# Expert weights of a two-block transformer kernel in another HBM layout

## The chip, the cores and the metric

The kernel runs on one core of one Trainium2 chip, in float32 throughout; many products are made of two float32r parts. The metric is the device time of one execution in microseconds, the median of several. PE is TensorE, ACT ScalarE, DVE VectorE, POOL GpSimd and SP SyncE. A row names a line of the kernel as L963, and the releaser of a wait stands behind an arrow.

## What is computed

The reference chains two transformer blocks over 256 tokens of width 1024. The first has two kinds of attention heads, a mixture of 32 experts with 4 chosen per token, and an embedding gate; the second has block attention, a linear recurrence and a feed-forward net. The part that the change touches is the mixture of experts:

```
logits = xt @ w_router + b_router;  top_logit, top_e = lax.top_k(logits, 4);  gate = softmax(top_logit)
# per expert e, over the tokens xs that chose it:
hh = jnp.dot(xs, w_gu[e]) + b_gu[e]                    # (1024, 2048) weights
glu, lin = jnp.split(hh, 2, axis=-1)                   # clipped at 7
act = glu * jax.nn.sigmoid(1.702 * glu) * (lin + 1.0)
y = jnp.dot(act, w_dn[e]) + b_dn[e]                    # (1024, 1024) weights, then times gate and summed per token
```

Every expert's weights are 12.6 MB, so all 32 together are 403 MB of the 480 MB that the kernel reads.

## The kernel before

**Stages.** First mixer (to about 150 us), routing (to 165), experts (to about 1118), embedding gate and second mixer (to about 1260), feed-forward net (to the end).

**Weights as a stream.** All large weights come in chunks of up to 2 MB, a tile of 128 partitions with 16 KB each. `plan` (L165 on, filled by `want`) lists them in the order of use: for expert `e` four chunks `("gu", e, c)`, then the two chunks `("dn", e - 1, c)` of the expert before it. `load_next` (L213) takes the next entry and issues its transfer on SP's queue; two chunks of the last experts go over POOL's queue (L228), and the very last as two halves (L231). `done(key)` is called when the last matmul of a chunk stands in the program; it gives the buffer back and calls `load_next` for the same ring. Three rings hold the buffers: `ringa` with three, `ringb` with five until expert 30, `ringc` with one, so nine chunks can be landed or under way. A transfer waits on SP until its buffer is free, and SP handles the plan in order.

The chunks of `w_gu` and `w_dn` are cut out of the weights as the reference has them, by rearranged views:

```
wg = A["w_gu"].rearrange("e (c k p) n -> e c p k n", p=P, k=2)   # L182: partition p gets rows p and 128 + p, 8 KB each
wd = A["w_dn"].rearrange("e (c k p) n -> e c p k n", p=P, k=4)   # L183: four rows, 4 KB each
```

Other weights (`w_in`, `w_in2`, `w_up`) are already permuted on the host, in `host_arrays`, so that a partition's 16 KB are one run.

**An expert on the engines.** `gather` (L939 to L951) picks the expert's up to 64 tokens by a one-hot product; `up` (L963) makes 64 matmuls over the four gu chunks, two column halves of the array at a time; ACT copies the result out, `glu` (L978) transposes it and DVE and ACT apply the gate; `down` (L999) makes 32 matmuls over the two dn chunks; `scatter` (L1027) adds the rows back to the tokens. The loop runs the `up` of expert e + 1 before the `down` of expert e. `past_slots` (L1056) stands between `up` and `down` of the last experts: a branch on the largest count of tokens (L1059, L1060) around a loop that reloads weights in small pieces for tokens past the 64 slots.

The order of instructions on each engine is drawn up when the program is built, by a planner that orders by priority and by estimated durations; `tc.issue_after` pins it in a few places, none in the loop over experts up to expert 29.

Of the kernel before, what the change touches and what calls it, by code (L numbers as in the profile page):

```python
# [36 lines left out]
P = 128  # L37
S = 256
D = 1024
# [9 lines left out]
# ---------------------------------------------------------------- constants of the shapes  # L49
# [3 lines left out]
def _const_pack():  # L53
    cols, parts, at = {}, [], 0

    def put(name, a):
        nonlocal at
        a = np.asarray(a, np.float32)
        cols[name] = (at, a.shape[1])
        parts.append(a)  # L60
        at += a.shape[1]

    i = np.arange(P)
    r, c = i[:, None], i[None, :]
    put("ident", r == c)
    put("flip", r + c == P - 1)
    put("iotad", np.broadcast_to(c % CAP, (P, P)))
    put("iota32", np.broadcast_to(np.arange(E)[None, :], (P, E)))
    put("comb", (r < 64) & (r % 32 == c % 32))
    put("masksb", np.where(c >= r, NEG, 0.0))  # L70
    put("maskml", np.where(c > r, NEG, 0.0))
    put("upper", r < c)
    # distance 255 - m of a row of the relative bias, m = 0 .. 383
    n = np.arange(384)
    dist = 255 - n
    nn = np.maximum(dist, 0)
    nf = np.maximum(nn, 1).astype(np.float32)
    large = 16 + (np.log(nf / np.float32(16)) / np.float32(math.log(8.0)) * np.float32(16)).astype(np.int32)
    bucket = np.where(nn < 16, nn, np.minimum(large, 31))
    oh = np.zeros((P, 384), np.float32)  # L80
    oh[bucket, n] = 1.0
    oh[:, dist < 0] = 0.0
    put("bucket", oh)
    put("maskd", np.broadcast_to(np.where(dist < 0, NEG, 0.0)[None, :], (P, 384)))
    return cols, np.ascontiguousarray(np.concatenate(parts, axis=1))
# [6 lines left out]
# columns of the per-partition vectors  # L92
# [11 lines left out]
def block_kernel(ctx: ExitStack, tc: tile.TileContext, A, out, dbg=None, parts=("t1", "moe", "over", "t3")):  # L104
# [36 lines left out]
    # ------------------------------------------------------------ constants  # L141
# [22 lines left out]
    # ------------------------------------------------------------ weights that stream  # L164
# [17 lines left out]
    wg = A["w_gu"].rearrange("e (c k p) n -> e c p k n", p=P, k=2)  # L182
    wd = A["w_dn"].rearrange("e (c k p) n -> e c p k n", p=P, k=4)  # L183
# [63 lines left out]
    # ------------------------------------------------------------ helpers  # L247
    def split(pool, src, tag="w", eng=V):
        """src in two float32r parts."""
        shape = [P] + list(src.shape[1:])  # L250
        hi = pool.tile(shape, FR, name=tag + "h")
        lo = pool.tile(shape, FR, name=tag + "l")
        act(hi, src)
        eng.tensor_tensor(out=lo, in0=src, in1=hi.bitcast(FT), op=OP.subtract)  # L254
        return hi, lo

    def tiles_T(key):
        """the column tiles of a transposed product: (chunk key, half, tile)."""
        return [(key, hf, m) for hf in range(2) for m in range(2)]
# [25 lines left out]
    def sq_mean(o, src, junk):  # L285
        """the share of 512 columns in the mean of 1024 squares."""
        act(junk, src, AF.Square, scale=1.0 / 32.0, accum_out=o)
# [7 lines left out]
    def rms_halves(o, src, small, junks=None):  # L295
        """1 / rms of the rows of src [128, 1024]."""
        ss = small.tile([P, 2], FT, name="ss2", bufs=4)
        for n in range(2):
            junk = junks(n) if junks else small.tile([P, 512], FT, name="junk", bufs=2)
            sq_mean(ss[:, n:n + 1], src[:, n * 512:(n + 1) * 512], junk)  # L300
        rs_sum(o, ss, small)

    def turn_tile(src, t, gcol, uh, ul, psum):
        """one token tile [128, 1024] transposed, times the gain column of each k tile, in two parts."""
        tl = slice(t * P, (t + 1) * P)
        for g in range(2):
            pt = psum()
            for k in range(4):
                PE.transpose(pt[:, k * P:(k + 1) * P], src[:, (4 * g + k) * P:(4 * g + k + 1) * P], ident)
            for k in range(4):  # L310
                kk = 4 * g + k
                pk = pt[:, k * P:(k + 1) * P]
                if k % 2 == 0:
                    act(uh[:, kk, tl], pk, AF.Copy, scale=gcol(kk))
                else:
                    ts(uh[:, kk, tl], pk, gcol(kk), None, OP.mult)
                stt(ul[:, kk, tl], pk, gcol(kk), uh[:, kk, tl].bitcast(FT), OP.mult, OP.subtract)

    def spread_tile(rB, r, t, small, psum):
        """rB [128, 256]: the column r of one token tile along the free axis, on every partition."""  # L320
        rb = small.tile([P, P], FT, name="rb", bufs=1)
        ts(rb, ones, r[:, t:t + 1], None, OP.mult)
        pb = psum()
        PE.matmul(pb[:, 0:P], rb, ident, start=True, stop=True)
        V.tensor_copy(rB[:, t * P:(t + 1) * P], pb[:, 0:P])
# [9 lines left out]
    # ============================================================ first mixer  # L335
# [31 lines left out]
    # constants that are not needed at once  # L367
# [12 lines left out]
    # ---- projections of the stick-breaking heads  # L380
# [46 lines left out]
    # rotary tables  # L427
# [30 lines left out]
    # ---- stick-breaking heads, and the latent projections between them  # L458
# [6 lines left out]
    def pair_out(o, which, p, gname):  # L465
        """the two parts of a pair of heads times its gain, and their squares."""
        k = 4 * which + p
        sq = t1l.tile([P, S], FT, name="sq", bufs=2)
        act(sq, o, AF.Square)
        act(mxh[:, k], o, AF.Copy, scale=vc(gname, p))  # L470
        stt(mxl[:, k], o, vc(gname, p), mxh[:, k].bitcast(FT), OP.mult, OP.subtract)
        if p == 0:
            sqs[which] = psc.tile([P, 2], FT, name="c")
        for t in range(2):
            PE.matmul(sqs[which][:, t:t + 1], sq[:, t * P:(t + 1) * P], ones[:, 0:1], start=(p == 0 and t == 0),
                      stop=(p == 3), skip_group_check=True)
        if p == 3:
            for t in range(2):
                rsq(hcol[:, 2 * which + t:2 * which + t + 1], sqs[which][:, t:t + 1], 512, t1l)
# [67 lines left out]
    # latent projections  # L547
# [7 lines left out]
    def latent(nk, ncol, gname, dst, wsplit_iter, last_done):  # L555
        """tokens by ncol, normalised, transposed into dst."""
# [49 lines left out]
    def mla_proj():  # L606
# [14 lines left out]
        # queries  # L621
# [48 lines left out]
    # half of -8 softplus(-lam)  # L670
# [10 lines left out]
    # rows of the relative bias by distance; the router's weights times their gain  # L681
# [19 lines left out]
    # ---- latent heads  # L701
# [39 lines left out]
    def half_o(which):  # L741
        """the product of one half of w_o, scaled by its norm."""
# [33 lines left out]
    # ============================================================ routing  # L776
# [30 lines left out]
    # the tokens transposed, for the router  # L807
# [46 lines left out]
    def gate_values():  # L854
# [13 lines left out]
        # what goes past the slots  # L868
# [23 lines left out]
    # three bfloat16 parts that add up to the tokens  # L892
# [30 lines left out]
    # ============================================================ experts  # L923
# [132 lines left out]
    def past_slots():  # L1056
        """pairs past the slots of their expert."""
        pacc = pc_.tile([P, 512], FT, name="sc")
        mv = nc.values_load(maxi[0:1, 0:1], min_val=0, max_val=S)  # L1059
        with tc.If(mv > CAP):  # L1060
            with ExitStack() as c5:
# [12 lines left out]
                with tc.For_i(0, E, 1) as e:  # L1074
                    cv = nc.values_load(cnti[0:1, ds(e, 1)], min_val=0, max_val=S)
                    with tc.If(cv > CAP):
                        with ExitStack() as c4:
# [6 lines left out]
                            for m in range(8):  # L1084
                                w = ov.tile([P, 8, 2, P], FT, name="ovw", bufs=2)
                                for s in range(2):
                                    SY.dma_start(w[:, :, s], A["w_gu"][ds(e, 1), :, s * 1024 + m * P:s * 1024 + (m + 1) * P]
                                                 .rearrange("o (k p) n -> p (o k) n", p=P))
# [13 lines left out]
                            for s in range(4):  # L1102
                                w = ov.tile([P, 8, 256], FT, name="ovw", bufs=2)
                                SY.dma_start(w, A["w_dn"][ds(e, 1), :, s * 256:(s + 1) * 256]
                                             .rearrange("o (k p) n -> p (o k) n", p=P))
# [37 lines left out]
    # the last two experts' rows meet in one accumulation  # L1143
# [20 lines left out]
    def row_split(key, i, gain=None):  # L1164
        """a k tile of weights, times the gain column, in two parts."""
# [19 lines left out]
    # ============================================================ gate of the embeddings, final norm  # L1185
# [8 lines left out]
    def nat2(keys, lhs, epilogue, pre, gain=None):  # L1194
        """[tokens, 1024] = lhs^T w; the last four k tiles go token tile by token tile."""
# [46 lines left out]
    def norm_rows(t, src, gain, o, res, last=None, part=None):  # L1242
        """rows of src normalised, times the gain row, added to res."""
# [61 lines left out]
    # ============================================================ second mixer  # L1305
# [46 lines left out]
    def lru_a(hf):  # L1352
        # r = (1 + tanh) / 2, log a = c8 r; 1 - a^2 = tanh(-log a) (1 + a^2)
# [198 lines left out]
    # ============================================================ feed forward  # L1552
# [68 lines left out]
# ---------------------------------------------------------------- host: layout only  # L1621
def host_arrays(inputs):
# [10 lines left out]
    def colchunks(a, n):  # L1633
        """(1024, m*n) -> [m][128][8*n]"""
# [3 lines left out]
    def pairs(a, n=256):  # L1638
        """chunks of two halves: [m/2][128][2][8*n]"""
# [3 lines left out]
    def rows(a):  # L1643
        """(1024, 512) -> [1][128][2][4*512]"""
# [24 lines left out]
    f["w_gu"] = c(g["w_gu"][0])  # L1669
    f["w_dn"] = c(g["w_dn"][0])  # L1670
# [60 lines left out]
```

## Time and profile before

| | us |
|---|---|
| median of the runs (lowest, highest) | 1460.15 (1459.87, 1460.45) |
| span of the profiled execution | 1458.6 |
| PE busy | 1346.5 (92%) |
| DVE busy | 633.4 (43%) |
| ACT busy | 370.8 (25%) |
| POOL busy | 40.5 (3%) |
| DMA, mean over the span | 330 GB/s |

The page gives no time of the profiled execution beside its span; the span stands 1.55 us under the median of the runs. The busy time of an engine is the union of its instructions. The DMA share is the mean over 16 DMA engines of the time that their packets took; packets can overlap, so it can exceed 1. The granted clock of PE is a share of its full 2.4 GHz; the lower level is 1.2 GHz.

### The profile page before, as it was taken

Reading aid. Unit: us, or ns where it says so; the run is one execution under the profiler, and the core shown is the slowest. Engines: PE = TensorE matmul, PEld = TensorE weight load, DVE = VectorE, ACT = ScalarE, POOL = GpSimd, SP = SyncE. Lnnn points to the kernel's source line nnn. Section 1 sums busy time; section 2 is a strip of 40 time slices with the busy share of each in tenths; the row PEclk is TensorE's granted clock in tenths of the full one; section 3 lists DMA queues with packets and bytes.
Section 4 is the critical chain, followed back from the end, with each engine's and each line's share of the span. In section 5 each row is a group of like instructions: output and inputs, shape, how many; then the busy total and the mean of one; then the engine's idle time right before and its main releaser. Section 6 shows DMA issues by size and latency. Waiting matters only on the chain. (4 is left out here: it accounts for less than half of the span.)

```text
span 1458.6 us, 19750 instructions
## 1 busy us (share of the span) xinstructions
PE 1346.5 (92%) x8361; PEld 747.0 (51%) x8362; DVE 633.4 (43%) x1250; ACT 370.8 (25%) x639; POOL 40.5 (3%) x54
## 2 busy tenths in 40 slices
PE   6999999999999999999899889899897999999997
PEld 6877533433333333333333333333333897799997
DVE  5676422332233223322332223222224878777776
ACT  5545210100100010001000010000113647465554
POOL 1010200000000000000000000000000101000000
PEclk9999999999999999999999999999999999999999
DMA  7238799999999999999999999999997543344540
GB/s 276 109 129 365 280 417 417 415 415 417 417 417 415 416 417 416 418 415 416 417 416 418 415 416 417 416 417 415 405 385 304 196 175 131 118 186 183 201 165 29
DMA packets 82380, 481.91 MB, mean 330 GB/s; under 512 B 4104, under 2 KB 5792, under 8 KB 46448
## 3 DMA queue, kind: packets, MB, share of 16 engines
q1 hardware_dynamic: 79616, 472.93, 80.4%
q0 software_dynamic: 1808, 6.55, 1.2%
q8 instruction: 67, 1.10, 0.3%
q10 hardware_dynamic: 864, 1.13, 0.3%
q14 instruction: 25, 0.20, 0.0%
HBM read 479.53 MB, written 1.06 MB: 329 GB/s over the span
## 5 line engine op out<-in xcount | busy, mean ns | idle before, releaser
L963 PE MATMUL gu<-w,xg 128*64 128x512 f32 x2048 | 476.3, 616 | 16.4 <-DMA w<-w_gu 15.8
L963 PEld LDWEIGHTS gu<-w,xg 128*64 128x64 f32 x2048 | 143.8, 141 | 312.6 <-issue 275.9
L999 PE MATMUL y<-w,gl 128*64 128x512 f32 x1024 | 238.7, 603 | 9.4 <-PEq L1060 6.1
L120 ACT ACTIVATE h<-gu,gs 128x512 f32<-128x512 f32 x64 | 40.5, 683 | 579.6 <-PE gu L963 579.6
L254 DVE TENSOR_TENSOR wl<-w,wh 128x1024 fp32r<-128x1024 f32 (+2 forms) x124 | 148.0, 1205 | 46.8 <-ACT wh L120 46.3
L120 ACT ACTIVATE wh<-w 128x1024 fp32r<-128x1024 f32 (+2 forms) x125 | 128.1, 1038 | 96.5 <-PE acc L272 21.0
L123 DVE TENSOR_TENSOR xg<-xg,vec 128x512 f32<-128x512 f32 x32 | 22.1, 691 | 283.1 <-PE gu L963 279.8
L999 PEld LDWEIGHTS y<-w,gl 128*64 128x64 f32 x1024 | 69.6, 137 | 129.5 <-issue 121.1
L123 DVE TENSOR_TENSOR h<-sc,h 128x512 f32<-128x512 f32 x126 | 81.6, 686 | 117.2 <-PE sc L1027 113.5
L271 PE MATMUL wk<-ul,wh 128*128 128x256 f32 x336 | 94.5, 281 | 0.2 <-DVE ul L123 0.2
L270 PE MATMUL wk<-uh,wh 128*128 128x256 f32 x336 | 94.5, 281 | 0.0
L272 PE MATMUL wk<-uh,wl 128*128 128x256 f32 x336 | 94.3, 281 | 0.0
L126 DVE SCALAR_TENSOR_TENSOR sg<-y,gs,li 128x512 fp32r<-128x512 f32 x31 | 23.3, 751 | 125.2 <-ACT li L120 125.2
L120 ACT ACTIVATE li<-y,gs 128x512 fp32r<-128x512 f32 x31 | 21.3, 687 | 194.1 <-PE y L999 194.1
L939 PEld LDWEIGHTS <-u 128*128 128x128 bf16 x1536 | 54.3, 98 | 28.0 <-issue 27.4
L271 PEld LDWEIGHTS wk<-ul,wh 128*128 128x128 f32 x336 | 63.4, 189 | 1.2 <-DVE ul L123 0.4
L270 PEld LDWEIGHTS wk<-uh,wh 128*128 128x128 f32 x336 | 63.3, 188 | 1.0 <-ACT uh L120 0.2
L272 PEld LDWEIGHTS wk<-uh,wl 128*128 128x128 f32 x336 | 63.4, 189 | 0.0
L978 PE MATMUL tr<-cf,h 128*128 128x128 f32 x256 | 39.3, 286 | 23.6 <-ACT h L120 23.4
L939 PE MATMUL xg<-oh,u 128*128 128x64 bf16 x1536 | 59.6, 193 | 0.7 <-ACT proj L120 0.7
L123 DVE TENSOR_TENSOR gl<-tr,bgu 128x512 f32<-128x512 f32 x32 | 22.1, 691 | 71.3 <-PE tr L978 71.3
L978 PEld LDWEIGHTS tr<-cf,h 128*128 128x128 f32 x256 | 26.8, 140 | 51.3 <-ACT h L120 49.2
(410 smaller groups left out, 1750.8 us busy)
## 6 DMA issues: line engine op xcount, KB each, us to landing
w<-w_gu SPq DMA_DIRECT2D x128, 2048.0 KB, 25.9
w<-w_dn SPq DMA_DIRECT2D x61, 2048.0 KB, 30.7
w<-w_up SPq DMA_DIRECT2D x11, 2048.0 KB, 8.9
w<-w_in SPq DMA_DIRECT2D x7, 2048.0 KB, 10.3
w<-w_down SPq DMA_DIRECT2D x5, 2048.0 KB, 7.4
w<-w_o SPq DMA_DIRECT2D x4, 2048.0 KB, 8.9
w<-w_dn POOLq DMA_DIRECT2D x2, 2048.0 KB, 14.4
w<-w_pg SPq DMA_DIRECT2D x2, 2048.0 KB, 9.3
```

What stands on the lines that cost most here:

```text
L120: return SC.activation(out=o, in_=i, func=f, **kw)
L123: return V.tensor_tensor(out=o, in0=a, in1=b, op=op)
L126: return V.scalar_tensor_tensor(out=o, in0=a, scalar=s, in1=b, op0=op0, op1=op1)
L254: eng.tensor_tensor(out=lo, in0=src, in1=hi.bitcast(FT), op=OP.subtract)
L270: PE.matmul(o, l[0], r[0], start=first, stop=False)
L271: PE.matmul(o, l[0], r[1], start=False, stop=False)
L272: PE.matmul(o, l[1], r[0], start=False, stop=last)
L939: PE.matmul(px[:, kd], u3[i][:, t, kd * P:(kd + 1) * P], oh[:, t], start=(n == 0), stop=(n == 5))
L963: PE.matmul(ps[64 * s:64 * s + 64, n], xg[:, k], w[:, kk, s * 1024 + n * 512:s * 1024 + (n + 1) * 512], start=(k == 0), stop=(k == 7))
L978: PE.transpose(pt[:, m], hf[:, m * P:(m + 1) * P], ident)
L999: i = PE.matmul(ps[64 * s:64 * s + 64], aT[:, k], w[:, kk, s * 512:(s + 1) * 512], start=(k == 0), stop=(k == 7))
```

## The change

The host permutes `w_gu` and `w_dn` into chunks as they lie in SBUF: `w_gu` becomes (32, 4, 128, 2, 2048), `w_dn` (32, 2, 128, 4, 1024). The two rearranged views in the kernel fall away, and each chunk's transfer reads one run of 16 KB per partition. `past_slots` reads small pieces of the same weights by expert and column; each of its transfers is split by chunk (four for `w_gu`, two for `w_dn`). Comments are removed and leave empty lines. Nothing else differs.

```
-    wg = A["w_gu"].rearrange("e (c k p) n -> e c p k n", p=P, k=2)
-    wd = A["w_dn"].rearrange("e (c k p) n -> e c p k n", p=P, k=4)
+    wg, wd = A["w_gu"], A["w_dn"]
...
                                 for s in range(2):
-                                    SY.dma_start(w[:, :, s], A["w_gu"][ds(e, 1), :, s * 1024 + m * P:s * 1024 + (m + 1) * P]
-                                                 .rearrange("o (k p) n -> p (o k) n", p=P))
+                                    for c in range(4):
+                                        SY.dma_start(w[:, 2 * c:2 * c + 2, s],
+                                                     wg[ds(e, 1), c, :, :, s * 1024 + m * P:s * 1024 + (m + 1) * P]
+                                                     .rearrange("o p k n -> p (o k) n"))
...
-                                SY.dma_start(w, A["w_dn"][ds(e, 1), :, s * 256:(s + 1) * 256]
-                                             .rearrange("o (k p) n -> p (o k) n", p=P))
+                                for c in range(2):
+                                    SY.dma_start(w[:, 4 * c:4 * c + 4], wd[ds(e, 1), c, :, :, s * 256:(s + 1) * 256]
+                                                 .rearrange("o p k n -> p (o k) n"))
...
-    f["w_gu"] = c(g["w_gu"][0])
-    f["w_dn"] = c(g["w_dn"][0])
+    f["w_gu"] = c(g["w_gu"][0].reshape(E, 4, 2, P, 2 * D).transpose(0, 1, 3, 2, 4))
+    f["w_dn"] = c(g["w_dn"][0].reshape(E, 2, 4, P, D).transpose(0, 1, 3, 2, 4))
```

## Rows read from the trace of the kernel before

**Rows 1.** The page: span, and GB/s in 40 equal slices.

```profile
span 1458.6 us, 19750 instructions
...
GB/s 276 109 129 365 280 417 417 415 415 417 417 417 415 416 417 416 418 415 416 417 416 418 415 416 417 416 417 415 405 385 304 196 175 131 118 186 183 201 165 29
```

**Rows 2.** Stretches: length, engines' busy us (instructions), PEclk, DMA share, GB/s.

```profile
300.00:700.00 400.00, 374.28 (x2304) 145.61 (x2300) 117.47 (x245) 35.46 (x55) 0.00 (x0) 0.97 1.02 416
700.00:1030.00 330.00, 293.47 (x1792) 111.95 (x1790) 93.62 (x194) 28.40 (x44) 0.00 (x0) 0.98 1.02 416
```

**Rows 3.** The page's DMA issues: count, KB each, us to landing.

```profile
w<-w_gu SPq DMA_DIRECT2D x128, 2048.0 KB, 25.9
```

**Rows 4.** Waits of PE, 200 to 703 us (all), then 703 to 1073 (longest).

```profile
PE sc L1027 <- ACT li L120: 12.6, 16, 0.8
PE tr L978 <- ACT h L120: 12.6, 15, 0.8
PE y L945 <- DVE sg L126: 4.7, 17, 0.3
...
PE gu L963 <- DMA w<-w_gu: 15.8, 18, 2.9
```

**Rows 5.** Timeline of PE: start, us, instructions; first chunk of experts 7, 8, 9.

```profile
355.22 3.65 PE L963 MATMUL gu<-w,xg 128*64 128x512 f32 x16
...
383.37 5.35 PE L963 MATMUL gu<-w,xg 128*64 128x512 f32 x16
...
413.19 3.65 PE L963 MATMUL gu<-w,xg 128*64 128x512 f32 x16
```

**Rows 6.** Stretches around the long chunk of expert 8.

```profile
366.00:383.30 17.30, 15.39 (x118) 6.76 (x114) 5.46 (x11) 2.58 (x4) 0.00 (x0) 1.00 1.01 416
383.40:388.70 5.30, 5.30 (x20) 1.46 (x18) 1.75 (x6) 0.00 (x0) 0.00 (x0) 0.68 1.03 410
```

**Rows 7.** Timeline of PE: chunks of experts 19, 24, 24, 25 and 30.

```profile
703.11 3.65 PE L963 MATMUL gu<-w,xg 128*64 128x512 f32 x16
...
855.25 3.65 PE L963 MATMUL gu<-w,xg 128*64 128x512 f32 x16
...
868.33 3.65 PE L963 MATMUL gu<-w,xg 128*64 128x512 f32 x16 [1.33 <-DMA w<-w_gu]
...
885.36 5.35 PE L963 MATMUL gu<-w,xg 128*64 128x512 f32 x16
...
1037.57 3.65 PE L963 MATMUL gu<-w,xg 128*64 128x512 f32 x16
```

**Rows 8.** Timeline of PE, 1050 to 1103 us: expert 30, then the branch.

```profile
1050.64 3.65 PE L963 MATMUL gu<-w,xg 128*64 128x512 f32 x16 [1.34 <-DMA w<-w_gu]
...
1060.99 3.65 PE L999 MATMUL y<-w,gl 128*64 128x512 f32 x16 [0.93 <-DMA w<-w_dn]
...
1102.78 5.88 PE L999 MATMUL y<-w,gl 128*64 128x512 f32 x14 [6.07 <-PEq L1060]
```

**Rows 9.** Stretches of one run length: w_gu (8 KB), then w_o (4 KB).

```profile
120.00:140.00 20.00, 20.00 (x114) 14.63 (x114) 13.94 (x42) 11.17 (x33) 0.00 (x0) 1.00 1.01 422
...
79.00:83.00 4.00, 4.00 (x31) 3.51 (x30) 2.71 (x7) 1.49 (x4) 0.00 (x0) 0.88 1.00 410
```

**Rows 10.** Stretches of w_in (16 KB), and the packets from 15 to 23 us.

```profile
15.00:23.00 8.00, 7.54 (x38) 7.15 (x39) 4.82 (x13) 7.45 (x16) 1.11 (x2) 1.00 1.01 429
...
16.00:22.00 6.00, 5.97 (x27) 5.89 (x28) 3.18 (x9) 5.45 (x13) 1.11 (x2) 1.00 1.00 426
...
DMA packets 229, 3.43 MB, mean 429 GB/s; under 512 B 19, under 2 KB 19, under 8 KB 19
```

**Rows 11.** Timeline of PE: first chunks of experts 1 and 2.

```profile
185.71 13.95 PE L963 MATMUL gu<-w,xg 128*64 128x512 f32 x64
...
211.86 13.95 PE L963 MATMUL gu<-w,xg 128*64 128x512 f32 x64
```

**Rows 12.** A stretch in which w_in's transfers run beside others.

```profile
1130.00:1135.00 5.00, 5.00 (x23) 4.09 (x23) 4.59 (x4) 3.50 (x4) 0.39 (x1) 1.00 0.98 357
```

## Prediction

> **What bounds the kernel now.** The page comes first. It gives the profiled execution a span of 1458.6 us, 1.55 us under the 1460.15 us median of the runs; I take what lies around the span as constant, so a step that shortens the span by x takes x off the median. The slices of the page show one long middle, 23 of 40, at 415 to 418 GB/s [rows 1]: the expert stage. There the stretches read a DMA share of 1.02 at 416 GB/s, first half and second half alike, with PE busy for 374 of 400 us and then 293 of 330 [rows 2]. So both resources are nearly full, and the question is which of them ends last. A w_gu chunk needs 25.9 us from issue to landing [rows 3] though its 2 MB take 5 us at that rate: some five chunks stand in the queue, and the transfers never pause.
>
> The waits decide it. Between 200 and 703 us PE waits for ACT and DVE alone, never for a weight; between 703 and 1073 us it waits for w_gu 18 times [rows 4]. The stage therefore has two halves with different bounds. In the first, PE paces itself: expert 7 begins at 355.22, expert 8 at 383.37, expert 9 at 413.19 [rows 5], periods of 28.15 and 29.82 us. The two differ by one chunk of 16 matmuls that takes 5.35 us where others take 3.65: over 383.4 to 388.7 the granted clock is 0.68, a piece at 1.2 GHz among 2.4 GHz, after 17.3 us in which PE was busy for 15.4 at a clock of 1.00 [rows 5, 6]. That falls in every second expert from the sixth to the eighteenth, so PE's own pace is a mean of 28.99 us per expert. In the second half DMA sets the pace: expert 24 begins at 855.25, expert 25 at 885.36, 30.11 us, with a wait of 1.33 us for w_gu inside [rows 7].
>
> Why the waits start only at expert 19: nine ring buffers are full when the experts begin, and PE, faster than the stream by 30.25 - 28.99 = 1.26 us per expert, eats that stock. (30.25 us is one expert's 12.583 MB at 416 GB/s.)
>
> **The change, part by part.** *The plan's views* lose their rearrange: the same 192 chunks of 2 MB, same order, same buffers, same 128 partitions; each partition's 16 KB is one run where it was two of 8 KB (w_gu) or four of 4 KB (w_dn). No instruction is added or removed outside the branch of past_slots. *past_slots* gets 52 more DMA instructions in a body that this input doesn't enter: no load of it stands in the trace, and the 6.07 us that PE idles at that branch [rows 8] stay; between nothing and 0.5 us for a longer jump, and I take nothing. *The host* permutes before the launch: outside the time.
>
> What a run's length is worth on the chip has three readings in this trace. A stretch of w_gu chunks alone, 120 to 140 us, moves 422 GB/s; w_o chunks in 4 KB runs move 410 GB/s [rows 9]. The w_in chunks at the start already lie with 16 KB per partition: 15 to 23 us moves 429 GB/s, 16 to 22 us 426. In those 8 us 229 packets carry 3.43 MB, and 19 of them are under 512 B: the other 210 are 16.3 KB each, so a 16 KB run does go as one packet, and under a full queue [rows 10]. I take 429, the longer stretch, with 426 as the lower end; above it the trace shows nothing, and as will be seen a higher rate would not show in the time. At 429 GB/s an expert's 12.583 MB take 29.33 us (29.54 at 426) against 30.25 before: 0.92 us per expert, 0.153 us per chunk.
>
> The Trainium skill's page "DMA: Bandwidth & Descriptors", section "Why small descriptors are slow (HBM only)", speaks against so much: it gives a fixed overhead of about 3 cycles per packet and finds packing worthwhile only at descriptors of 256 B or less. By its figures (32 B per cycle, 850 MHz) an expert's packets would take 0.96% less, an estimate from that page, 0.29 us per expert in place of 0.92, and the kernel would come out near 1451 us, as at the lower rate of the second rival. The trace's steps from 410 to 422 to 429 GB/s are larger than that rule allows.
>
> Now who uses the 0.92 us. A faster stream can't speed PE where PE doesn't wait, so experts 0 to 18 stay as they are and expert 19 still begins at 703.11 [rows 7]. From there PE can run at its own pace: 11 periods to expert 30, six of 28.15 and five of 29.82, 318.0 us, so expert 30 begins at 1021.1 in place of 1037.57 [rows 7]: **16.5 us**. Inside expert 30 the waits of 1.34 us for w_gu and 0.93 us for w_dn [rows 8] go too: **2.3 us**. Together 18.8 us.
>
> Does the stream keep up with that? Its hardest point is expert 30's last w_gu chunk, which PE waited for at 1050.64 [rows 8]. At its own pace PE wants it at 1021.1 + 11.2 = 1032.3 (the three chunks before it and the scatter among them, 3.65 us each and 0.66), 18.3 us sooner. About 168 chunks flow without a pause before it, so each has to gain 0.109 us: a rate of 425 GB/s is enough. At 429 the chunk lands 168 x 0.153 = 25.7 us sooner, 7.4 us ahead of need; at 426 just in time. So of 25.7 us only 18.8 show: DMA stops being what ends last, and PE's pace takes its place. Behind expert 30 I find no wait of the tail for w_gu or w_dn, so it moves forward whole.
>
> Forecast: span 1458.6 - 18.8 = 1439.8, time 1460.15 - 18.8 = **1441.4 us**.
>
> **The rivals.** *One, PE's order changes.* The order of instructions is drawn up when the program is built, by a planner with estimated durations, and another layout may change its estimates. The experts are not all ordered alike: expert 1 to expert 2 took 185.71 to 211.86, 26.15 us [rows 11], with the gather placed where it hides PE's waits for ACT. If that order came to hold throughout, DMA would stay the bound and all 25.7 us and the 0.93 would show: 1433.5 us. Against it: bytes, count and order of the loads stay the same. 8%.
>
> *Two, the run's length is worth less.* If a 16 KB run goes no faster than an 8 KB one, only w_dn gains: 6 chunks at 422 GB/s are 29.82 us per expert, 0.072 us per chunk, 12.0 us by expert 30's last chunk; with the 0.93 that is 1447 us. At 420 GB/s it is 8.1 and 0.93: 1451 us. The same comes out if the change doesn't do what it says and the long run is cut into 8 KB packets; the 16.3 KB per packet speak against it. 12%.
>
> *Three, long packets get in each other's way under load: slower.* In 1130 to 1135 us, where w_in's 16 KB packets run beside other loads, a DMA share of 0.98 moves only 357 GB/s [rows 12]: an expert would take 35.2 us, a chunk 0.83 us more than now, and 168 of them 140 us: some 1600 us. It decides as soon as the rate falls below 416 GB/s. Against it: loads start on idle engines in that stretch, and the stretch at a full queue [rows 10] shows no such thing. 3%.
>
> *Four, PE's pace gets worse* (an order with one more wait for ACT, or the low clock in every expert). The low clock in all 11 would give 328.0 in place of 318.0 us, a gain of 8.8: 1451; an order worse by 1.5 us per expert would eat all of it. 7%, more than half of it within 0.2% of now or slower.
>
> **How the numbers follow.** The forecast has 70%. Its own lower end: without any fall of the clock the 11 periods are 309.7 us, a gain of 27.1 us, of which the stream allows 26.6: 1433.5 us. The range runs from 1433 to 1450: it takes in the forecast, rival one and the better half of rival two, and leaves out the other half, three and four. About 0.2% (3 us) is what a measurement of this kernel can tell from no change. Faster 0.91, same 0.05, slower 0.04.
>
> **What would show it.** Right: about 429 GB/s between 300 and 700 us; some 24,700 packets for w_gu and w_dn where their runs now make 65,500; no wait of PE for either; expert 19 beginning near 703 as before; periods of 28.15 and 29.8 us up to expert 30; and a stock that lasts, so that chunks land before they are wanted. Wrong: waits for w_gu that remain after 900 us (the step of the rate), experts before 19 that begin at other times (the step of the order), a rate at or under 422 (rival two), a period other than 28.15 without a wait or a low clock (rival four).

## The result and the profile after

The changed kernel takes 1438.1 us (median of 4 runs, 1437.8 to 1439.1) where the kernel before takes 1460.3: a ratio of 0.985, 95% interval 0.984 to 0.987. The forecast was 1441.4 us, in a range of 1433 to 1450. Two further measurements of the same two kernels on other chips gave 0.988 (0.985 to 0.990) and 0.986 (0.985 to 0.987). Between the medians the three gains are 22.2, 19.6 and 21.2 us, against the 18.8 forecast. Of the 12 executions of the changed kernel the two fastest (1435.0 and 1435.4 us) show a mean granted clock of 0.981 and the two slowest (1443.5 and 1443.7) one of 0.975, so gains that differ by two or three us may differ by the clock alone. The profiled execution of after took 1437.77 us, 1.77 of them around its span.

From the page of the changed kernel: the span, the engines' busy time, GB/s in 40 slices, all packets, and the packets of SP's queue (count, MB, share of the 16 engines).

```profile
span 1436.0 us, 19750 instructions
PE 1342.9 (94%) x8361; PEld 748.1 (52%) x8362; DVE 633.5 (44%) x1250; ACT 371.0 (26%) x639; POOL 40.1 (3%) x54
...
GB/s 281 111 126 375 275 428 426 428 427 426 427 426 427 427 427 427 426 427 428 426 427 426 427 428 426 426 429 426 395 382 306 176 150 132 132 181 199 200 154 30
DMA packets 41549, 481.92 MB, mean 336 GB/s; under 512 B 4104, under 2 KB 5792, under 8 KB 13680
...
q1 hardware_dynamic: 39552, 472.93, 79.5%
```

The same queue's row on the page of before:

```profile
q1 hardware_dynamic: 79616, 472.93, 80.4%
```

The same bytes, and 40,064 packets fewer; with the 768 that POOL's queue saved (1808 before, 1040 after) it is 40,832. That is 32 experts x 16 DMA engines x 80 (128 packets per engine and expert before, 48 after) less 128, which are the pieces of 8 KB in which the very last chunk, issued as two halves, still goes. So the long runs did go as one packet each. The long middle of the slices stands at 426 to 428 GB/s where it stood at 415 to 418 [rows 1].

Two stretches of the middle (length, busy us of PE, PEld, DVE, ACT and POOL, PEclk, DMA share, GB/s), to be laid beside [rows 2]:

```profile
300.00:700.00 400.00, 373.25 (x2296) 145.35 (x2292) 117.96 (x246) 36.14 (x56) 0.00 (x0) 0.97 1.01 427
700.00:1000.00 300.00, 280.81 (x1710) 109.45 (x1712) 88.95 (x187) 25.81 (x40) 0.00 (x0) 0.97 1.01 427
```

In the first, PE is as busy as before (373 of 400 us, 374 before): there it gained nothing from the faster stream. The second is the one that changed: 94% busy where it was 89%.

The waits of PE say why; all of them from 200 to 703 us, then all from 703 to 1060 us (us in total, times, longest):

```profile
PE sc L1026 <- ACT li L120: 12.6, 16, 0.8
PE tr L977 <- ACT h L120: 12.6, 15, 0.8
PE y L944 <- DVE sg L126: 4.8, 17, 0.3
...
PE tr L977 <- ACT h L120: 10.1, 12, 0.8
PE sc L1026 <- ACT li L120: 8.7, 11, 0.8
PE y L944 <- DVE sg L126: 3.2, 11, 0.3
```

The first three are those of [rows 4] (lines are numbered one lower now). The 18 waits for w_gu behind 703 us, 15.8 us of them, are gone: no wait for a weight is left in the whole stage.

The timeline of PE (start, us, instructions): the first chunks of experts 18 to 21 and of expert 30, the rest of expert 30, the first chunk of expert 31, and the chunk behind the branch.

```profile
671.37 5.35 PE L962 MATMUL gu<-w,xg 128*64 128x512 f32 x16
...
701.21 3.65 PE L962 MATMUL gu<-w,xg 128*64 128x512 f32 x16
...
729.35 5.35 PE L962 MATMUL gu<-w,xg 128*64 128x512 f32 x16
...
759.20 3.65 PE L962 MATMUL gu<-w,xg 128*64 128x512 f32 x16
...
1019.25 5.35 PE L962 MATMUL gu<-w,xg 128*64 128x512 f32 x16
...
1025.19 10.52 PE L962 MATMUL gu<-w,xg 128*64 128x512 f32 x48
...
1037.82 7.09 PE L998 MATMUL y<-w,gl 128*64 128x512 f32 x32
...
1053.61 5.35 PE L962 MATMUL gu<-w,xg 128*64 128x512 f32 x16
...
1080.24 5.32 PE L998 MATMUL y<-w,gl 128*64 128x512 f32 x14 [3.22 <-PEq L1059]
```

The pattern of the first half [rows 5], 28.15 and 29.82 us in turn, now runs on through expert 30: 28.14 us (701.21 to 729.35), then 29.85 (729.35 to 759.20). In expert 30 the chunks go in one run of 48 and one of 32 matmuls where [rows 8] shows waits between them.

Where the 22.6 us of span went, from first matmul to first matmul:

| stretch | before | after | gained |
|---|---|---|---|
| start to expert 0 | 167.6 | 165.6 | 1.9 |
| expert 0 to expert 30 | 870.0 | 853.6 | 16.4 |
| expert 30 to expert 31 | 35.8 | 34.4 | 1.5 |
| expert 31 to the end | 385.2 | 382.4 | 2.8 |

(Gains are taken before rounding.) The middle two rows are the change. In the other two PE waits for none of these weights in these two profiles. A part of the first can be seen in a stretch of the prelude; 155 to 160 us, of before and then of after:

```profile
155.00:160.00 5.00, 5.00 (x12) 2.65 (x12) 3.95 (x19) 1.90 (x6) 1.84 (x2) 0.66 0.86 364
```

```profile
155.00:160.00 5.00, 4.21 (x15) 1.75 (x14) 4.96 (x25) 2.38 (x7) 1.16 (x1) 1.00 0.56 239
```

In before, PE was granted a clock of 0.66 there, in after 1.00; the same two values stand over 75 to 80 us. The last row of the table is the wait at the branch, 6.07 us in [rows 8] and 3.22 above.

### The profile page after: what moved, and what is told of

The parts are those of the page before. It is cut to its first block, busy times and chain, and to the rows that moved or that the text cites. A ratio compares the mean times of both kernels' runs of the same rounds, so it can differ in the third digit from the quotient of the medians.

```text
span 1436.0 us, 19750 instructions
## 1 busy us (share of the span) xinstructions
PE 1342.9 (94%) x8361; PEld 748.1 (52%) x8362; DVE 633.5 (44%) x1250; ACT 371.0 (26%) x639; POOL 40.1 (3%) x54
## 3 DMA queue, kind: packets, MB, share of 16 engines
q0 software_dynamic: 1040, 6.55, 1.2%
## 5 line engine op out<-in xcount | busy, mean ns | idle before, releaser
L962 PEld LDWEIGHTS gu<-w,xg 128*64 128x64 f32 x2048 | 147.0, 142 | 293.7 <-issue 292.5
```

Of the source, the lines that this page charges most:

```text
L962: PE.matmul(ps[64 * s:64 * s + 64, n], xg[:, k], w[:, kk, s * 1024 + n * 512:s * 1024 + (n + 1) * 512], start=(k == 0), stop=(k == 7))
```

## The experiments

My theory: the length of a packet sets the rate of the stream, and with the new layout PE's pace, carried by the full buffers, is what ends last. The rivals to it: that the chunk's place in HBM, one piece of 2 MB, gives the rate and not the run's length; that the gain came from PE (another order, or the clock); and that the two outer terms of the table belong to the change.

**The kernel before, once more.** One execution of the unchanged kernel, for the size of what varies by itself.

> The kernel before, once more, for a second profile. The step of the prediction that came out short is the part outside the experts (about 3.6 of 22.5 us of span): the first profile of before has two pieces at the low clock ahead of the experts and a long one at the branch of past_slots, the profile of after has none ahead. If these pieces lie by chance, a second profile of before puts them elsewhere, by some 1 to 3 us. If they belong to the kernel, it shows them where the first did: one near 77 us, one near 155 us, one near 1101 us.

It took 1465.75 us, 6.5 more than the median of 13 executions of this kernel on the same chip, and more than the longest of them (1461.4). The stretch shown above, in this execution:

```profile
155.00:160.00 5.00, 5.00 (x11) 2.74 (x11) 3.76 (x17) 1.53 (x6) 1.90 (x2) 0.50 0.84 354
```

The granted clock there is at 1.2 GHz throughout, a second such piece stood near 76 us (0.66 over 75 to 80, as in the first profile), the first expert began at 169.3 in place of 167.6, and the branch wait was 5.6 us. Behind expert 31 PE also waited 2.35 us for w_dn, which the first profile does not have. So the low pieces ahead of the experts stand where they stood, but the outer terms still move by a few us between executions of one program. It is a single execution.

**The same place in HBM, short runs.** Of the changed kernel the host alone and the view differ: the same chunk order, with 256 B of gap behind each row, so that no 8 KB or 4 KB run joins the next.

```
-    wg, wd = A["w_gu"], A["w_dn"]
+    wg, wd = A["w_gu"][:, :, :, :, 0:2 * D], A["w_dn"][:, :, :, :, 0:D]
...
+    f["w_gu"] = c(np.pad(gu, ((0, 0),) * 4 + ((0, 64),)))
+    f["w_dn"] = c(np.pad(dn, ((0, 0),) * 4 + ((0, 64),)))
```

> The order of the kernel after in HBM, but 256 B of gap behind every row, so that a partition's 16 KB are again two runs of 8 KB (w_gu) or four of 4 KB (w_dn). If the length of a run is what counts: 416 GB/s in the experts, waits for w_gu from about expert 19 on, the time of before, 1458 to 1462 us. If it is the neighbourhood in HBM (one partition's rows side by side): 427 GB/s and 1437 to 1440 us.

1460.9 us, a ratio of 1.001 (1.000 to 1.003) to before. The stretch 300 to 700 us, and PE's waits for w_gu from 200 to 1000 us:

```profile
300.00:700.00 400.00, 371.36 (x2292) 144.44 (x2292) 117.49 (x245) 35.49 (x55) 0.00 (x0) 0.97 1.02 417
...
PE gu L962 <- DMA w<-w_gu: 19.0, 21, 2.6
```

The rate of before and its waits are back, and the whole gain is gone, though the chunks lie in the order in which the change put them, each in one piece but for the gaps. The run's length is the cause; having a chunk's bytes together in HBM gives nothing here.

**One weight alone.** The new layout for w_gu alone, then for w_dn alone; the other keeps its old view and layout.

```
-    wg, wd = A["w_gu"], A["w_dn"]
+    wg, wd = A["w_gu"], A["w_dn"].rearrange("e (c k p) n -> e c p k n", p=P, k=4)
```

> Only w_gu in the new layout, w_dn in rows of 4 KB as before. If every packet costs the same bit of time whatever its length: 64 packets fewer of the 128 per engine and expert that the change saves in all (w_gu goes from 64 to 32, w_dn stays at 64), about 29.9 us per expert, 420 GB/s, waits for w_gu that begin late, 1447 to 1452 us. If only short runs cost: nothing, 1460 us.

> Only w_dn in the new layout, w_gu in rows of 8 KB as before. By a fixed cost per packet: w_dn goes from 64 to 16 packets per engine and expert, about 29.8 us per expert, 422 GB/s, 1444 to 1449 us, so more than w_gu alone gives. If only runs under 8 KB cost: all of the gain, 1438 us.

w_gu alone: 1450.4 us, 0.994 (0.992 to 0.996). w_dn alone: 1446.9 us, 0.992 (0.990 to 0.993). The stretch and the wait for w_gu (200 to 1000 us) of w_gu alone, with the first chunks of two experts in a row:

```profile
300.00:700.00 400.00, 373.21 (x2296) 145.43 (x2293) 117.64 (x246) 36.15 (x56) 0.00 (x0) 0.97 1.01 421
...
PE gu L962 <- DMA w<-w_gu: 5.5, 5, 1.3
...
967.36 3.65 PE L962 MATMUL gu<-w,xg 128*64 128x512 f32 x16
...
997.17 3.66 PE L962 MATMUL gu<-w,xg 128*64 128x512 f32 x16
```

and the stretch of w_dn alone:

```profile
300.00:700.00 400.00, 373.20 (x2308) 146.20 (x2308) 118.61 (x248) 36.18 (x56) 0.00 (x0) 0.97 1.01 422
```

Each half gives a rate between 416 and 427 and a part of the gain (9 and 12 us of some 20). w_dn moves half of w_gu's bytes and yields no less: per expert and engine its runs save 48 packets (64 to 16), w_gu's 32 (64 to 32), of 80 in all; the "64 packets fewer of the 128" in the first expectation is a miscount. The gain goes with the packets, not with the bytes. The second rival of the prediction, in which only w_dn gains, was put at 422 GB/s [rows 9] and 1447 us; w_dn alone gave 422 and 1446.9.

**All runs 4 KB long.** The same gap, behind every 4 KB.

```
-                want(("gu", e, c), wg[e, c], [P, 2, 2048])
+                want(("gu", e, c), wg[e, c].rearrange("p k s n -> p (k s) n"), [P, 4, 1024])
```

> All expert weights in runs of 4 KB (256 B of gap behind each), the order in HBM otherwise as in the kernel after: 192 packets per engine and expert where before has 128 and after 48. By a fixed cost per packet the expert takes about 30.8 us, 408 GB/s; since the stream already sets the end in the kernel before, all of it shows: 168 chunks by 0.1 us, 1474 to 1480 us, and waits for w_gu from about expert 13 on. If PE were the bound before: no change, 1460 us.

1476.4 us, 1.012 (1.010 to 1.013). The stretch, the waits (200 to 1000 us), and the first chunks of two experts:

```profile
300.00:700.00 400.00, 360.71 (x2208) 138.38 (x2206) 113.09 (x236) 33.60 (x52) 0.00 (x0) 0.98 1.02 409
...
PE gu L962 <- DMA w<-w_gu: 33.9, 30, 3.0
...
683.44 3.65 PE L962 MATMUL gu<-w,xg 128*64 128x512 f32 x16
...
714.11 3.65 PE L962 MATMUL gu<-w,xg 128*64 128x512 f32 x16
```

409 GB/s, next to the 410 of w_o's 4 KB runs in [rows 9], and a period of 30.67 us. Shorter runs cost what longer ones give back.

**The changed kernel again, twice,** on the two other chips, to have its time beside the experiments that follow.

> The kernel after, once more, timed beside the next three on one chip. The stream in the experts runs at 427 GB/s and PE never waits for a weight: a ratio of 0.984 to 0.988 to the kernel before (1437 to 1442 us). Its low-clock pieces ahead of the experts and at the branch may lie elsewhere than in the first profile and move the span by 1 to 3 us.

> The kernel after, timed beside the next two on one chip: a ratio of 0.984 to 0.988 to the kernel before, no wait of PE for an expert weight.

1440.9 and 1438.3 us, ratios as in the first paragraph; 427 GB/s and no wait for a weight in either. Their branch waits were 3.2 and 3.6 us, and both began expert 0 at 165.5. In the second, expert 0 to 30 took 853.6 us, as in the first profile of after.

**Less work for PE.** Two of the three bf16 parts in the gather's products are left out, in the changed kernel and in the one before. If the stream paces before and PE paces after, only the second should have something to win, until the stream stops it.

```
-                for i in range(3):
+                for i in range(1):
```

> The kernel before with the same two parts of the tokens left out of the gather. The stream sets its end, so PE's 1.2 us per expert don't show but for the first experts, ahead of a full queue: waits for w_gu begin near expert 10 in place of 19 and grow, 1455 to 1460 us. If PE were the bound there: 1420 us.

> The kernel after with two of the three bfloat16 parts of the tokens left out of the gather (16 in place of 48 small matmuls per expert), about 1.2 us less of PE per expert. By the prediction's sum the stream at 427 GB/s is only some 3 us ahead of PE at expert 30, so PE runs into the stream again: waits for w_gu come back from about expert 10 to 14 on, and of the 38 us that PE saves only 3 to 6 show, 1432 to 1436 us. If PE's pace were the bound with room to spare: 1400 to 1405 us.

Before without this work: 1459.2 us, 0.999 (0.998 to 1.000), nothing. Its stretch and its waits (200 to 1000 us):

```profile
300.00:700.00 400.00, 351.45 (x1829) 127.43 (x1826) 115.68 (x244) 36.19 (x56) 0.00 (x0) 0.99 1.02 417
...
PE gu L963 <- DMA w<-w_gu: 34.4, 34, 2.8
PE y L999 <- DMA w<-w_dn: 11.2, 19, 2.0
```

PE worked 23 us less in these 400 us and the time didn't move: what it saved it waited. After without this work: 1437.5 us (1433.8 to 1440.2), 0.985 (0.982 to 0.988), 3.5 us under its companion on the same chip, with intervals that overlap. The gain is the size expected (3 to 6), but not shown clear of noise, and the time lies above the 1432 to 1436 expected. Its waits (200 to 1000 us), and the first chunks of two experts:

```profile
PE gu L962 <- DMA w<-w_gu: 24.5, 30, 2.6
...
658.18 3.65 PE L962 MATMUL gu<-w,xg 128*64 128x512 f32 x16
...
687.57 3.65 PE L962 MATMUL gu<-w,xg 128*64 128x512 f32 x16
```

PE ran at 26.95 us per expert until the stock was eaten, from expert 13 on at the stream's 29.39. So at 427 GB/s the stream is still slower than PE's 28.99, and it is the stock that hides it up to the end.

**A smaller stock.** The changed kernel with seven ring buffers in place of nine.

```
-NRING_A, NRING_B = 3, 5
+NRING_A, NRING_B = 3, 3
```

> The kernel after with three buffers in ringb in place of five, so seven chunks of stock in place of nine: 9.8 us less. The stream needs 29.4 us per expert and PE 28.99, so in the kernel after it is the stock of the start that carries PE to expert 30, with some 3 us left by the sum. With 9.8 us less the stock ends near expert 17, waits for w_gu come back there, and the time is 5 to 8 us over the kernel after. If the stream outran PE by itself, the stock would not matter: the same time as the kernel after, no waits.

1446.8 us, 0.992 (0.990 to 0.994), 8.5 us over the changed kernel on the same chip (the ends of the two intervals leave 3 to 14). The stretch and the waits (200 to 1000 us):

```profile
300.00:700.00 400.00, 371.60 (x2316) 145.45 (x2312) 118.27 (x246) 36.14 (x56) 0.00 (x0) 0.99 1.01 427
...
PE gu L962 <- DMA w<-w_gu: 11.3, 12, 1.3
```

The same rate, but the waits for w_gu come back from expert 17 on, and with them periods of 29.38 us. Two chunks of stock are 2 x 29.39 / 6 = 9.8 us of lead; by the lower end of the interval, about a third of it at least was needed.

**PE's own pace, with another order.** The low clock of every second expert is part of PE's 28.99. I held the gather of expert e + 2 back behind expert e's last product, the place it has in experts 1 and 2 [rows 11], and hoped for 27.2 us per expert; then the same with the last gather left free.

```
-        down(e, aT)
+        i = down(e, aT)
...
-            gather(e + 2)
+            with tc.issue_after(i.ins):
+                gather(e + 2)
```

> The kernel after with the gather pinned behind the down product in the loop (its small matmuls then fill PE's wait of 0.79 us for ACT behind the down product), so PE's own period falls from 28.15 to about 27.2 us. PE is the bound in the kernel after, but the stream is only some 3 us behind it: the waits for w_gu come back from about expert 12 on and 2 to 4 us of the 30 us show, 1434 to 1438 us where the kernel after is at 1438 to 1441. If PE alone were the bound: 1410 us. If the kernel after has no slack left in the stream: no change.

> As after_pin, but the gather of the last expert keeps the place that it has in the kernel after. In after_pin expert 30 began 4.0 us sooner than in the kernel after, and expert 30's own stretch was 5.3 us longer, with the gather of expert 31 among its products. If that gather is what cost the 5.3 us, the 4 us remain: a ratio of 0.982 to 0.985 to the kernel before. If the stream is what holds expert 30 there, the ratio stays at 0.986 or above, with waits for w_gu inside expert 30.

1441.8 us, 0.988 (0.987 to 0.990), 3.5 us over the changed kernel on the same chip with intervals that just meet, and a miss (1434 to 1438 was expected); and 1439.2 us, 0.985 (0.982 to 0.987), on another chip, no different from the changed kernel's 0.985 to 0.988. The stretch of the first:

```profile
300.00:700.00 400.00, 378.01 (x2348) 148.16 (x2348) 122.12 (x254) 36.17 (x56) 0.00 (x0) 1.00 1.01 427
```

A granted clock of 1.00: the pieces at 1.2 GHz are gone, with PE busier than before (378 of 400 us, 373 in after). The period was 28.06, not 27.2, since in place of the wait for ACT stands one for DVE (17 times up to 703 us, 9.3 us in all). From expert 17 PE waited for weights again, at 29.39 us per expert: expert 0 to 30 took 849.5 us where after takes 853.6. Those 4.1 us are as far as PE got ahead before this stream held it. The first of the two lost it in expert 30 (38.5 us to expert 31, against 33.1), where the last gather now stood; the second lost less there (35.4) and had 5.7 us of branch wait. Neither is shown to beat the changed kernel.

## Why the prediction was right, and where it was off

**The rate.** 429 GB/s was forecast, 427 measured. Where a kernel's stream is the bound, the period of an expert without a low clock reads the stream directly: 30.67 us with 192 packets per engine and expert, 30.11 with the 128 of before [rows 7], 29.81 with 96 (w_gu alone), 29.39 with 48 (the new layout, less gather work). The ends give (30.67 - 29.39) / 144 = 8.9 ns per packet; by that line 128 packets make 30.10 and 96 make 29.82. With w_dn alone (80 packets, 29.67 by the line) PE showed 29.54 to 29.82 in those experts, no settled row of equal periods; the landings of its chunks settle at 29.68 to 29.73 us per expert. The forecast took its periods from the rates of two stretches, 30.25 us before and 29.33 after. The settled periods lie 0.72 us apart, where it had 0.92; most of the difference is the 429, since at the measured 427 the same reckoning gives 29.47 us and a gain of 0.78. The Trainium skill's page "DMA: Bandwidth & Descriptors", section "Why small descriptors are slow (HBM only)", gives about 3 cycles per packet, at the 850 MHz of the page's specifications an estimate of 3.5 ns. The runs don't agree: they show 8.9 ns, and the time of 1451 us that the prediction worked out by this page did not come.

**Who uses it.** Experts before the nineteenth were to stay as they were. They did: expert 19 began 535.6 us after expert 0, and 535.6 in before. From there 318.0 us to expert 30 were forecast and 318.04 measured (701.21 to 1019.25), 16.4 us less than before against 16.5. DMA stopped being what ends last, and PE's pace with its low clock took over. The 25.7 us that the stream was to allow were never there: with the pinned order, which the stream holds from expert 17 on, expert 0 to 30 is 20.5 us shorter than before (849.5 for 870.0).

**The slack.** The last w_gu chunk of expert 30 was put 7.4 us ahead of need. The trace has its issue on SP's queue in after (start, us), and its time to landing (count, KB, us):

```profile
994.79 0.33 SPq L232 DMA_DIRECT2D w<-w_gu  x1
...
w<-w_gu SPq DMA_DIRECT2D x1, 2048.0 KB, 33.4
```

It landed at 1028.2, and PE began it near 1032.1 (the last third of the run of 48 above): 4.0 us ahead, and 2.5 in each of the two further profiles of the changed kernel. The need was forecast rightly (1032.3). The term that was too large is the landing "25.7 us sooner": in before the chunk landed at 1050.6 [rows 8], 883.0 us after expert 0 began, in after 862.5, so 20.5 us sooner. That is 0.122 us on each of 168 chunks in place of 0.153. The sum needed 0.109, so its 18.8 us held by little. The transfers also don't run quite "without a pause": by the landings, some 1.5 us more are lost about once in six experts, before and after alike, so the stream's mean from expert 6 to 30 is 30.39 and 29.64 us per expert (0.75 apart), over the settled 30.11 and 29.39. What holds it there was not followed.

**Expert 30.** Its waits of 2.3 us were to go. They went, but its first chunk fell to 1.2 GHz (5.35 us for the 3.65 of [rows 7]), which took 1.7 us back; the net is 1.5, and the 0.9 us between that and 2.3 - 1.7 was not followed. The pattern of every second expert runs on, and which expert it meets was not reckoned. In the two further profiles it meets expert 29, and expert 30 takes 33.2 and 33.1 us, 2.6 and 2.7 less than before.

**The size that was off: what lies outside.** The sum was 18.8 and the medians give 22.2, the spans 22.6. The two terms of the change are 17.9 us; 4.7 us lie before expert 0 and behind expert 31, where the prediction had nothing. So of the 3.8 us by which the span beat the forecast, none is the change's own: its terms came out 0.9 under the forecast, and what lies outside gave the rest. The step "the 6.07 us that PE idles at that branch stay" failed: it was 3.22. Over the profiles of this case that wait was 6.1, 5.6 and 4.2 us in the layout of before (the last with less gather work), 3.2, 3.2 and 3.6 in the changed kernel, 3.9 to 5.7 in the others; the two other gathers on the new layout had 4.0 and 5.7. It varies between executions; whether the layout shares in it stays open, and no run shows what a longer jump costs.

The clock ahead of the experts is open too. Over 75 to 80 and 155 to 160 us both profiles of before are granted 0.66 or less, the three of the changed kernel 1.00. But the layout does not decide it: with the gaps, at the rate of before, the second stretch has 1.00, and with seven buffers or the gather pinned, on the new layout, the first has 0.66. The start of expert 0 ranged from 165.0 to 169.3 over the experiments, 165.0 with the layout of before and less gather work, and about 167 in four kernels on the new order in HBM. These terms may make the difference between 19.6 and 22.2 us in the three measurements, and no run separates them.

**The rivals.** One (the order changes): it didn't. Two (the length is worth less): refuted by 427 GB/s. Three (long packets slower): refuted by the same. Four (PE's pace worse): the periods are the same to 0.03 us.

## What to carry to other kernels

Where a stream is slow although DMA's share reads full, count its packets: here each cost 8.9 ns on its engine, and a layout on the host that makes one long run of each partition's bytes removed most of them, with the order of the loads and PE's work as they were. Then ask who uses the gain. With buffers full at the start, PE's waits for weights begin only when the stock is eaten, so the gain is bounded by those late waits and by PE's own pace, not by the bytes over the new rate. To price a faster stream, take the settled periods or the landings of like transfers: here the rate of another weight over 8 us (429 GB/s) promised 0.92 us per expert, and the runs gave 0.72 to 0.75.

## What the runs showed of the hardware

- The DMA share read 1.02 with runs of 4 KB (409 GB/s) and 1.01 with runs of 16 KB (427): it does not show what short packets cost.
- Of two orders with PE nearly always busy, the busier one (378 of 400 us, the gather behind the last product) was granted a clock of 1.00, the other (373 of 400) fell to 1.2 GHz for one chunk in every second expert. What tells them apart was not tried further.
- PE's idle time put down to the branch of past_slots, whose body this input does not enter, was between 3.2 and 6.1 us, differing by 2.5 us between executions of closely related programs, and by half a microsecond between two of the same one.
- Under a queue that is always full, each packet per DMA engine added 8.9 ns to the period of the stream beside its bytes: the periods with 192, 128, 96 and 48 packets, in runs of 4, 8 and 16 KB, lie on one line.
